# Own delays for the side steps of an emitted attention order, and wider tiles for the first adaLN weights

## The chip, the cores and the metric

The kernel runs on one core of one Trainium2 chip. The metric is the device time of one execution in microseconds (us). Within a core five engines work side by side: TensorE (PE, matrix products and transposes; its weight loads are listed apart as PEld), VectorE (DVE), ScalarE (ACT), GpSimd (POOL), and SyncE (SP), which in this kernel only issues transfers. Each engine works through its own list of instructions in order and waits at an instruction until what it needs is there.

## The reference, cut to what matters

Two layers of a hybrid backbone run over 640 tokens of width 1024: 128 context tokens and 512 latent tokens with shared weights. In each layer a conditioning vector is mapped to six modulation vectors (adaLN), one projection feeds three kinds of heads, and an output projection, a LayerNorm and an MLP follow.

```python
def _modulation(cvec, w_ada, b_ada):
    return jnp.split(jax.nn.silu(cvec) @ w_ada + b_ada, 6, axis=-1)
...
    h = x * (1.0 + sc_a) + sh_a
    mq, mk, mv, mo, mg, sq, sk, sv, nq, nk, nv = _split_in(h @ w_in + b_in)
    y_ml, _, _, _ = _mlstm_mixer(mq, mk, mv, mo, mg, fbias, norm_g, st_c, st_n, st_m)
    y_swa = _merge(_swa_latent(_rope_2d(_heads(sq, SWA_HEADS)), _rope_2d(_heads(sk, SWA_KV_HEADS)),
                               _heads(sv, SWA_KV_HEADS), ck_swa, cv_swa, sink))
    y_nat = _merge(_nat_latent(_heads(nq, NAT_HEADS), _heads(nk, NAT_HEADS), _heads(nv, NAT_HEADS),
                               ck_nat, cv_nat, rpb))
...
    mix = jnp.concatenate(mix_heads, axis=-1) @ w_out
    x = _layer_norm(DN_ALPHA * x + g_a * mix, ln1_g, ln1_b)
    h = x * (1.0 + sc_m) + sh_m
    f = jnp.square(jax.nn.relu(h @ w_mlp1)) @ w_mlp2
    return _layer_norm(DN_ALPHA * x + g_m * f, ln2_g, ln2_b)
```

The mLSTM scan carries a state from chunk to chunk, forward and backward; the context tokens hand their final state to the latent tokens. The outputs are both token streams, the context's keys and values, and the mLSTM states.

## The kernel before, in words

**Main stream.** Tokens are cut into five tiles of 128 (tile 0 is the context). Nearly all the work of TensorE is projections and MLP products: `gemm_feat` (L375, tile `gfeat`, features on the partitions) and `gemm_tok` (L306, tile `gtok`, tokens on the partitions). Every weight block arrives as `wrawt`, is split by ScalarE (L290) and VectorE (L291) into two parts `wst`, and each product is made of three matmuls.

**Side steps.** Everything else that TensorE does is cut into generators: the blocks of the neighbourhood heads (`nat`), of the window heads (`swa`) and of the mLSTM, the mLSTM's state recurrence (`chain`: `upd` L775, and on VectorE `mlst` L777), its closing (`finish`, `pty` L756), the context keys going out (`k_out`, `ptko` L863), the gates, the transposes back to features (`pth` L421), and adaLN (`ada`: load `adaw` L164, product `adaps` L169, bias add `adab` L183 on VectorE, transposes `adapt` L191). An attention block goes through scores `s` (L886), softmax on ScalarE and VectorE, transposes `ptp` (L929) and the product with the values `o` (L945).

**Order.** TensorE's list is written by hand. While the program emits the main stream it keeps a modelled time T; the steps lie in a queue with a ready time each, and after each piece of the main stream `pump` emits every eligible step whose ready time is not above T. The other engines' lists are set by a scheduler that follows data and buffers. All transfers are issued by SP in one list.

**First stage.** `start` computes the adaLN vectors that the first projection needs in four quarters. Each quarter takes eight 256 KB loads into eight `yp` buffers, its products, then the issue of the loads of the next quarter, which wait for these products to free the buffers.

**adaLN later on.** `ada` has one 1 MB buffer (`aw`), which `adaw`, the bias tile `adab` and the gate row share in turn. Each of the eight products of an `ada` is followed by the issue of the next load and a gap of modelled time; before the first product there is a load but no gap. In the MLP stages three of these run one after another.

**Output projection.** `tail1` makes it in two halves of 512 columns (`q` 0 and 1) with `by_block`: for each of eight row blocks k the tiles 0 to 2, later tiles 3 and 4, and the last block of all five at the end. The evacuation `ln_add` multiplies by the gate in place in PSUM (L1084) and adds to the residual `res` (L1088); the PSUM bank comes free with the second of these, and the second half needs the bank.

```python
            for k in range(7):
                blocks(k, range(3, NT))
            blocks(7, range(NT))
```

Of the kernel before, what the change touches and what calls it, by code (L numbers as in the profile page):

```python
# [9 lines left out]
F32 = mybir.dt.float32  # L10
# [20 lines left out]
YORDER = (0, 1, 5, 2, 6, 3, 7, 4)  # L31


class Net:
    def __init__(self, ctx, tc, I, O):
# [16 lines left out]
        self.queue, self.T = [], 0.0  # L52
# [11 lines left out]
    def add(self, gen, group, ready=0.0):  # L64
        self.queue.append([gen, group, max(self.T, ready)])
# [95 lines left out]
    def ada_load(self, pool, tag, l, i, q, n, k):  # L161
        w = pool.tile([128, 4, n], F32, tag=tag, name="adaw")
        src = self.I["w_ada0"][q, k] if l + i == 0 else self.I["w_ada"][3 * l + i - 1, q, k]
        self.nc.sync.dma_start(w, src.rearrange("p (j n) -> p j n", j=4))  # L164
        return w
# [32 lines left out]
    def ada(self, l, i, n, gap):  # L198
# [4 lines left out]
        ahead = [self.ada_load(self.adp, "aw", l, i, q, n, k) for q, k in todo[:1]]  # L203
        for m, (q, k) in enumerate(todo):
# [11 lines left out]
    def start(self):  # L216
# [5 lines left out]
        def load(q):  # L222
            w[q] = [self.ada_load(self.yp, "y", 0, 0, q, n, k) for k in range(8)]
# [75 lines left out]
    def gemm_tok(self, A, src, n, evac, by_block=False):  # L299
# [11 lines left out]
        if by_block:  # L311
# [24 lines left out]
            for k in range(7):  # L336
                blocks(k, range(3, NT))
            blocks(7, range(NT))
# [188 lines left out]
    def proj_ml(self, l, ms, pre=None):  # L527
# [11 lines left out]
        if ms[-1] == 3:  # L539
            self.ml_in = True  # L540
            self.ktok = self.yp.tile([128, 5, 256], F32, tag="y", name="ktok")
            self.add(self.ktok_prep(), "chain", self.use("A", 1.1, self.T + 0.3) + 0.1)
# [102 lines left out]
    def mlstm(self, l):  # L645
# [17 lines left out]
        def block(t):  # L663
# [67 lines left out]
            self.add(finish(t, hs), "fin", self.T + 2.4)  # L731
# [70 lines left out]
        for t in (0, 2, 3, 1, 4):  # L802
            self.add(block(t), "attn")
        self.add(chain(), "chain")
# [7 lines left out]
    def proj_qk(self, l, m, mode):  # L812
# [7 lines left out]
        if mode == "nk":  # L820
# [9 lines left out]
            self.add(self.k_out(kx, self.O["new_nat_k"][0, l, m - 4 : m - 2]), "kout", self.use("V", 0.3, f) + 0.1)  # L830
# [8 lines left out]
        else:  # L839
            for h in range(2):  # L840
                nc.scalar.activation(v[:, 0, h * 320 : (h + 1) * 320], g[h], AF.Identity, bias=b)
            if mode == "sk":
                kx = self.sm.tile([128, 128], F32, tag="kx", name="kxs", bufs=1)
                nc.vector.tensor_copy(kx, v[:, 0, 0:128])
                self.add(self.k_out(kx, self.O["new_swa_k"][0, l]), "kout", self.T + 2.5)
# [119 lines left out]
    def nat(self, l, u, qt, kt):  # L965
# [47 lines left out]
        for gen in [ctx_block()] + [block(cb) for cb in range(4)]:  # L1013
            self.s_left += 1
            self.add(gen, "attn", self.qk_ready)

    def swa(self, l, g, qt, kt, kc, vc):
# [52 lines left out]
        for gen in [ctx_block()] + [block(n) for n in range(4)]:  # L1070
            self.s_left += 1
            self.add(gen, "attn", self.qk_ready)
# [7 lines left out]
    def ln_add(self, r, q, o, gr, alpha, st=None):  # L1080
# [3 lines left out]
        nc.vector.tensor_tensor(out=o, in0=o, in1=gr[:, qs], op=ALU.mult)  # L1084
# [299 lines left out]
```

## Time and profile before

| | |
|---|---|
| median of 3 runs | 1780.16 us (1779.94 to 1780.73) |
| profiled execution | 1785.14 us |
| its span, first to last instruction | 1783.3 us |
| mean granted TensorE clock | 0.968 |
| TensorE busy | 1673.5 us (94% of the span) |
| VectorE busy | 958.7 us (54%) |
| ScalarE busy | 660.7 us (37%) |
| GpSimd busy | 187.8 us (11%) |

The time of the profiled execution and its span differ by 1.84 us, which lies around the recorded instructions. The first layer's attention runs from about 60 to 385 us, its MLP from about 415 to 940 us; the second layer's from about 945 to 1285 us and from about 1315 us to the end. The clock column of the profile is relative: 1.00 is TensorE's upper level of 2.4 GHz and 0.50 its lower of 1.2 GHz.

### The profile page before, as it was taken

What the parts mean: (1) busy time and instruction counts of PE and PEld (TensorE: products, weight loads), DVE (VectorE), ACT (ScalarE), POOL (GpSimd) and SP (SyncE); (2) the same over time, 40 slices, a digit from 0 to 9 for tenths busy, and PEclk for the clock granted to TensorE, in tenths of its full rate; (3) what the DMA queues carried; (4) which work ended last, traced back from release to release, by engine and by line L of the source; (5) the groups of instructions that cost most, each with busy time, mean ns of one, the idle gap of its engine ahead of it and who ended that gap; (6) DMA issues with size and microseconds to landing.
All of it is one profiled execution on the core that took longest, in us unless ns stands there. A gap on an engine that the chain in (4) does not pass through costs nothing.

```text
span 1783.3 us, 27709 instructions
## 1 busy us (share of the span) xinstructions
PE 1673.5 (94%) x10708; PEld 1453.3 (81%) x10708; DVE 958.7 (54%) x2105; ACT 660.7 (37%) x1482; POOL 187.8 (11%) x152
## 2 busy tenths in 40 slices
PE   5989898989999899999999897999899999999996
PEld 4879687868978777879988895888689898898985
DVE  3366766668633233234386787665685343433438
ACT  2342465645412212313253424666454142231320
POOL 1051000000201100101100510000003011020110
PEclk9998799999999999999999996999999999999998
DMA  8653442332344534422224331212413131321312
GB/s 280 223 157 122 165 131 90 106 119 78 108 152 159 172 130 165 166 78 94 63 77 143 106 110 36 64 58 76 130 60 104 50 101 43 105 78 53 98 45 83
DMA packets 107584, 195.24 MB, mean 109 GB/s; under 512 B 16666, under 2 KB 43290, under 8 KB 102332
## 3 DMA queue, kind: packets, MB, share of 16 engines
q1 hardware_dynamic: 107452, 193.47, 33.7%
q8 instruction: 84, 1.38, 0.3%
q14 instruction: 48, 0.39, 0.1%
HBM read 185.16 MB, written 8.26 MB: 108 GB/s over the span
## 4 chain that ended last, share of the span: by engine, by line
PE 75%; DVE 10%; DMA 5%; ACT 5%; issue 3%; SPq 0%; POOL 0%; DVEq 0%; ACTq 0%; POOLq 0%
PE gtok L306 34%; PE gfeat L375 31%; PE adaps L169 2%; ACT P L900 2%; PE o L945 2%; PE ptp L929 2%; DMA adaw<-in_w_ada 2%; DVE nm L893 2%; PE s L886 1%; PE mli L706 1%; DVE P L907 1%; DVE wst L291 1%; ACT PT L937 1%; DMA nbias<-in_nbias 1%; DMA adab<-in_b_ada 1%
## 5 line engine op out<-in xcount | busy, mean ns | idle before, releaser
L375 PE MATMUL gfeat<-Xt,wst 128*128 128x320 f32 x4416 | 688.1, 315 | 3.0 <-ACT f L1170 1.3
L375 PEld LDWEIGHTS gfeat<-Xt,wst 128*128 128x128 f32 x4416 | 660.6, 191 | 26.5 <-issue 16.6
L306 PE MATMUL gtok<-wst,f1T 128*128 128x512 f32 x1920 | 453.9, 397 | 1.8 <-POOL f1T L1175 1.2
L306 PEld LDWEIGHTS gtok<-wst,f1T 128*128 128x128 f32 x1920 | 361.6, 189 | 95.0 <-issue 7.5
L291 DVE TENSOR_TENSOR wst<-wrawt,wst 128x512 fp32r<-128x512 f32 (+2 forms) x392 | 272.8, 705 | 287.9 <-ACT wst L290 286.8
L290 ACT CAST wst<-wrawt 128x512 fp32r<-128x512 f32 (+2 forms) x392 | 232.5, 604 | 519.0 <-PE gtok L306 305.5
L1175 POOL TENSOR_TENSOR f1T<-f,f1T 128x640 fp32r<-128x640 f32 x64 | 103.4, 1615 | 1003.3 <-ACT f1T L1174 997.8
L1084 DVE TENSOR_TENSOR gtok<-gtok,row 128x512 f32<-128x512 f32 x100 | 69.4, 697 | 226.9 <-PE gtok L306 226.7
L306 PE MATMUL gtok<-wst,yT 128*128 128x512 f32 x480 | 120.3, 406 | 8.5 <-DVE res L1088 8.5
L306 PE MATMUL gtok<-wst,Xt 128*128 128x384 f32 (+1 forms) x720 | 122.1, 324 | 1.8 <-ACT wst L290 1.6
L306 PEld LDWEIGHTS gtok<-wst,Xt 128*128 128x128 f32 x720 | 113.0, 188 | 5.3 <-ACT wst L290 1.8
L306 PEld LDWEIGHTS gtok<-wst,yT 128*128 128x128 f32 x480 | 90.7, 193 | 30.4 <-DVE res L1088 9.4
L1170 ACT COPY f<-gfeat 128x320 f32<-128x320 f32 x128 | 54.3, 426 | 162.7 <-PE gfeat L375 158.0
L900 ACT ACTIVATE P<-P,nm 128x512 f32<-128x512 f32 (+2 forms) x120 | 80.6, 673 | 34.8 <-DVE nm L895 18.4
L169 PE MATMUL adaps<-adaw,cs 128*32 128x512 f32 (+1 forms) x576 | 60.0, 513 | 29.0 <-DMA adaw<-in_w_ada 28.3
L1171 DVE SCALAR_TENSOR_TENSOR f<-f 128x640 f32<-128x640 f32 x64 | 52.7, 823 | 52.7 <-ACT f L1170 52.7
L893 DVE TENSOR_REDUCE nm<-P 128x2 f32<-128x1024 f32 (+2 forms) x60 | 66.5, 1108 | 15.1 <-ACT P L982 8.5
L929 PE MATMUL ptp<-ident,P 128*128 128x128 f32 x432 | 65.5, 290 | 7.1 <-DVE P L907 5.9
L937 ACT COPY PT<-ptp 128x512 f32<-128x512 f32 (+1 forms) x120 | 60.9, 541 | 23.8 <-PE ptp L929 23.1
L424 ACT ACTIVATE val<-pth,affB,affA 128x128 f32<-128x128 f32 x120 | 45.5, 465 | 55.2 <-PE pth L421 55.2
L929 PEld LDWEIGHTS ptp<-ident,P 128*128 128x128 f32 x432 | 50.7, 147 | 16.9 <-issue 9.9
L1174 ACT CAST f1T<-f 128x640 fp32r<-128x640 f32 x64 | 46.6, 728 | 35.5 <-DVE f L1171 35.5
(208 smaller groups left out, 1282.4 us busy)
## 6 DMA issues: line engine op xcount, KB each, us to landing
wrawt<-in_w SPq DMA_DIRECT2D x256, 256.0 KB
adaw<-in_w_ada SPq DMA_DIRECT2D x40, 1024.0 KB
wrawt<-in_w_f SPq DMA_DIRECT2D x56, 256.0 KB
adaw<-in_w_ada SPq DMA_DIRECT2D x32, 256.0 KB
wrawt<-in_w_o SPq DMA_DIRECT2D x32, 256.0 KB
Dt<-md SPq DMA_DIRECT2D x40, 128.0 KB
nbias<-in_nbias SPq DMA_DIRECT2D x18, 256.0 KB
row<-adar SPq DMA_DIRECT2D x8, 512.0 KB
```

The source lines that it names most:

```text
L169: self.nc.tensor.matmul(ps[32 * j : 32 * j + 32, :], lhsT=self.cs[:, k, :], rhs=w[:, j, :], start=(k == 0), stop=(k == 7))
L290: nc.scalar.copy(ws[:, 0, :], raw)
L291: nc.vector.tensor_tensor(out=ws[:, 1, :], in0=raw, in1=ws[:, 0, :].bitcast(F32), op=ALU.subtract)
L306: nc.tensor.matmul(o, lhsT=A[YORDER[k] if A is self.Y else k][:, hl, t * 128 : (t + 1) * 128], rhs=ws[k][:, wl, :], start=(k == 0 and hl + ...
L375: nc.tensor.matmul(g[i, h], lhsT=w[i][k // 4][:, wl, (k % 4) * 128 : (k % 4 + 1) * 128], rhs=self.Xt[:, k, hl, h * 320 : (h + 1) * 320], s ...
L893: nc.vector.tensor_reduce(out=nm[:, 0:2], in_=P[:, :, 0:nk], axis=AX.X, op=ALU.max, negate=True)
L900: nc.scalar.activation(P[:, h, 0:nk], P[:, h, 0:nk], AF.Exp, bias=nm[:, h : h + 1], accum_out=nm[:, 2 + h : 3 + h])
L929: nc.tensor.transpose(pt[:, j, :], P[:, h, i * 128 : (i + 1) * 128], self.ident)
L937: nc.scalar.copy(dst, src)
L1084: nc.vector.tensor_tensor(out=o, in0=o, in1=gr[:, qs], op=ALU.mult)
L1170: nc.scalar.copy(f[:, h], g[h])
L1175: nc.gpsimd.tensor_tensor(out=y[:, 1], in0=f, in1=y[:, 0].bitcast(F32), op=ALU.subtract)
```

## The change

Four edits. (1) A table `LATER` of 63 named steps shifts the ready time of single steps, in tenths of a microsecond of modelled time; every step that is added gets a name (`0ml4` is layer 0, mLSTM, tile 4). (2) The first stage's adaLN weights are laid out so that one load brings two row blocks (512 KB instead of 256 KB) and a quarter takes four `yp` buffers instead of eight; the loads of quarter 1 are issued before quarter 0's products, those of quarter q+2 behind quarter q's. (3) `ada` yields once, for 8 us of modelled time, between its first load and its first product. (4) In the output projection the last block of tiles 0 to 2 comes as soon as its input is there, at the latest before the last block of tiles 3 and 4, and in the first half the gate product goes to an SBUF tile `wov`.

```diff
+LATER = {
+    "0": {7: -10, 8: 4},
...
+    "1ml4": {0: 102, 1: 27},
...
+    def add(self, gen, group, ready=0.0, name=""):
+        s = [gen, group, 0.0, f"{self.l}{name}", 0]
+        s[2] = max(self.T, ready) + self.later(s)
+        self.queue.append(s)
+
+    def later(self, s):
+        return 0.1 * LATER.get(s[3], {}).get(s[4], 0)
...
                         s[2] = max(self.T, ready)
+                        if cost > 0:
+                            s[4] += 1
+                            s[2] += self.later(s)
...
         ahead = [self.ada_load(self.adp, "aw", l, i, q, n, k) for q, k in todo[:1]]
+        yield 0.0, self.T + 8.0
         for m, (q, k) in enumerate(todo):
...
         def load(q):
-            w[q] = [self.ada_load(self.yp, "y", 0, 0, q, n, k) for k in range(8)]
+            w[q] = []
+            for k in range(4):
+                t = self.yp.tile([128, 2, 4, n], F32, tag="y", name="adaw")
+                nc.sync.dma_start(t, I["w_ada0"][q, k].rearrange("p (a j n) -> p a j n", a=2, j=4))
+                w[q] += [t[:, 0], t[:, 1]]
...
                 next(first)
+                load(1)
             for k in range(8):
                 self.ada_mm(ps[:, q, :], w[q][k], k)
-            if q < 3:
-                load(q + 1)
+            if q < 2:
+                load(q + 2)
...
-            for k in range(7):
+            late = True
+            for k in range(8):
                 blocks(k, range(3, NT))
-            blocks(7, range(NT))
+                if late and (k == 6 or (self.ydone[YORDER[7]] >= NT and self.yready[YORDER[7]] <= self.T)):
+                    late = False
+                    blocks(7, range(3))
...
-    def ln_add(self, r, q, o, gr, alpha, st=None):
+    def ln_add(self, r, q, o, gr, alpha, st=None, v=None):
...
-        nc.vector.tensor_tensor(out=o, in0=o, in1=gr[:, qs], op=ALU.mult)
+        v = o if v is None else v
+        nc.vector.tensor_tensor(out=v, in0=o, in1=gr[:, qs], op=ALU.mult)
+        o = v
...
-                self.ln_add(r, q, o, g[:, int(t == 0)], ALPHA, st[t] if q else None)
+                v = None if q else self.sm.tile([128, 512], F32, tag="val", name="wov", bufs=2)
+                self.ln_add(r, q, o, g[:, int(t == 0)], ALPHA, st[t] if q else None, v)
```

The names `L244`, `L266`, `L387`, `L459`, `L505` of the changed kernel are `L169`, `L191`, `L306`, `L375`, `L421` of the one before (the table pushes the lines down); `L767`, `L790`, `L796`, `L859`, `L947` are `L683`, `L706`, `L712`, `L775`, `L863`. In these lists a matmul on plain 32-bit floats stands once, where the trace has two records for it (`adaps` x4 there is x8 in the trace).

**First MLP, where one `ada` ends and the next begins (TensorE).** `adapt` are the last transposes of the first `ada`; the load of the next one is issued with them.

```order
L375 MATMUL gfeat<-Xt,wst 128x320 x60
L169 MATMUL adaps<-adaw,cs 32x512 x4
L375 MATMUL gfeat<-Xt,wst 128x320 x84
L191 MATMUL adapt<-ident,adab 128x128 x4
L375 MATMUL gfeat<-Xt,wst 128x320 x6
L169 MATMUL adaps<-adaw,cs 32x512 x4
```

The same place in the changed kernel:

```order
L459 MATMUL gfeat<-Xt,wst 128x320 x54
L244 MATMUL adaps<-adaw,cs 32x512 x4
L459 MATMUL gfeat<-Xt,wst 128x320 x78
L266 MATMUL adapt<-ident,adab 128x128 x4
L459 MATMUL gfeat<-Xt,wst 128x320 x72
L244 MATMUL adaps<-adaw,cs 32x512 x4
```

Between the transposes and the first product that needs the new load stood 6 matmuls of the main stream; now 72 stand there.

**First layer, the end of attention and the output projection (TensorE), before.** `o` is the last attention product, `pth` the transposes of a finished token tile; the first half of the output projection ends inside the long row.

```order
L945 MATMUL o<-PT,vc 64x128 x4
L306 MATMUL gtok<-wst,yT 128x512 x108
L421 MATMUL pth<-ident,res 128x128 x8
L306 MATMUL gtok<-wst,yT 128x512 x12
L421 MATMUL pth<-ident,res 128x128 x8
```

The same place in the changed kernel:

```order
L1029 MATMUL o<-PT,vc 64x128 x4
L387 MATMUL gtok<-wst,yT 128x512 x96
L505 MATMUL pth<-ident,res 128x128 x8
L387 MATMUL gtok<-wst,yT 128x512 x18
L505 MATMUL pth<-ident,res 128x128 x8
```

The number of products is the same; tiles 0 to 2 of each half are finished 12 matmuls sooner, and the transposes of their results come sooner with them.

**First layer, the mLSTM's recurrence (TensorE), before.** `mls` and `mli` are the block's products, `upd` the state updates, `ptko` transposes the context keys.

```order
L775 MATMUL upd<-mscr,ktok 64x65 x4
L375 MATMUL gfeat<-Xt,wst 128x320 x6
L775 MATMUL upd<-mscr,ktok 64x65 x4
L169 MATMUL adaps<-adaw,cs 32x512 x4
L863 MATMUL ptko<-ident,kxs 128x128
L375 MATMUL gfeat<-Xt,wst 128x320 x6
L706 MATMUL mli<-vaug,Dt 128x65 x4
L712 MATMUL mli<-mlst,mq 128x130 x4
L706 MATMUL mli<-vaug,Dt 128x65 x4
L775 MATMUL upd<-mscr,ktok 64x65 x4
```

The same place in the changed kernel:

```order
L859 MATMUL upd<-mscr,ktok 64x65 x4
L459 MATMUL gfeat<-Xt,wst 128x320 x6
L859 MATMUL upd<-mscr,ktok 64x65 x4
L459 MATMUL gfeat<-Xt,wst 128x320 x18
L790 MATMUL mli<-vaug,Dt 128x65 x4
L796 MATMUL mli<-mlst,mq 128x130 x4
L790 MATMUL mli<-vaug,Dt 128x65 x4
L859 MATMUL upd<-mscr,ktok 64x65 x4
L947 MATMUL ptko<-ident,kxs 128x128
L459 MATMUL gfeat<-Xt,wst 128x320 x18
L244 MATMUL adaps<-adaw,cs 32x512 x4
```

The transposes of the context keys and the `ada` product moved behind the block's products, and 18 main-stream matmuls instead of 6 stand ahead of these.

Further places of both attention stages move in the same way. One is on VectorE, where the bias add of a first-layer `ada` now stands between two steps of an mLSTM block (`num` is its numerator):

```order
L802 TENSOR_TENSOR num<-mli,mscr 128x260
L258 TENSOR_TENSOR adab<-adaps,adab 128x512
L803 TENSOR_TENSOR num<-num,mli 128x260
```

In the kernel before, the bias add stood among small steps of the gate norm and eight rows ahead of the first of that block's `num` rows.

## Rows read from the trace of the kernel before

**Rows 1.** The page: busy time and share by engine, and granted clock in 40 slices.

```profile
PE 1673.5 (94%) x10708; PEld 1453.3 (81%) x10708; DVE 958.7 (54%) x2105; ACT 660.7 (37%) x1482; POOL 187.8 (11%) x152
PEclk9998799999999999999999996999999999999998
```

**Rows 2.** The page: the chain that ended last, shares of the span by engine.

```profile
PE 75%; DVE 10%; DMA 5%; ACT 5%; issue 3%; SPq 0%; POOL 0%; DVEq 0%; ACTq 0%; POOLq 0%
```

**Rows 3.** Waits of PE: line, what ended them: total us, times, longest us.

```profile
PE adaps L169 <- DMA adaw<-in_w_ada: 28.3, 8, 7.8
PE gtok L306 <- DVE res L1088: 8.5, 2, 4.8
...
PE o L945 <- DVE yT L963: 5.5, 4, 4.1
PE ptko L863 <- DVE mlst L777: 5.3, 1, 5.3
PE pty L756 <- POOL hs L752: 5.1, 1, 5.1
...
PE gtok L306 <- POOL f1T L1175: 1.2, 1, 1.2
```

**Rows 4.** Windows at half clock: length, PE, PEld, DVE, ACT, POOL, clock, DMA, GB/s.

```profile
131.50:145.00 13.50, 12.15 (x57) 11.60 (x58) 8.11 (x33) 1.65 (x3) 3.06 (x5) 0.50 0.56 182
193.00:203.00 10.00, 10.00 (x57) 7.07 (x53) 6.19 (x18) 2.12 (x5) 0.00 (x0) 0.50 0.70 233
...
398.00:401.00 3.00, 3.00 (x9) 2.32 (x8) 3.00 (x7) 0.62 (x1) 0.00 (x0) 0.50 0.00 0
585.50:588.50 3.00, 3.00 (x15) 1.97 (x8) 0.00 (x0) 0.00 (x0) 0.00 (x0) 0.50 0.30 55
678.00:684.00 6.00, 5.80 (x17) 3.37 (x18) 0.00 (x0) 0.00 (x0) 0.00 (x0) 0.50 0.46 158
...
sum 94.00, PE 85.99 PEld 69.85 DVE 61.94 ACT 23.62 POOL 7.55; mean PE 5.37 PEld 4.37 DVE 3.87 ACT 1.48 POOL 0.47
```

**Rows 5.** Timeline, first MLP: start, duration, engine, operation, idle before and its releaser.

```profile
579.63 7.33 SPq L164 DMA_DIRECT2D adaw<-in_w_ada  x2
...
585.00 1.60 PE L169 MATMUL adaps<-adaw,cs 128*32 128x512 f32 x8 [4.53 <-DMA adaw<-in_w_ada]
...
596.55 1.06 PE L169 MATMUL adaps<-adaw,cs 128*32 128x512 f32 x8
...
678.20 1.94 PE L169 MATMUL adaps<-adaw,cs 128*32 128x512 f32 x8 [3.56 <-DMA adaw<-in_w_ada]
```

**Rows 6.** Timeline of PE, second layer: 72 main-stream matmuls in one row.

```profile
1338.69 11.05 PE L375 MATMUL gfeat<-Xt,wst 128*128 128x320 f32 x72 [0.52 <-ACT f L1170]
```

**Rows 7.** Timeline, first layer, between the halves of the output projection.

```profile
396.14 1.28 DVE L1088 SCALAR_TENSOR_TENSOR res<-res,gtok 128x512 f32<-128x512 f32 x2
...
397.47 2.78 PE L306 MATMUL gtok<-wst,yT 128*128 128x512 f32 x6 [4.83 <-DVE res L1088]
```

**Rows 8.** Timeline of PE, first stage: the first product of the second quarter.

```profile
18.60 1.31 PE L169 MATMUL adaps<-adaw,cs 128*32 128x128 f32 x16 [3.83 <-DMA adaw<-in_w_ada]
```

**Rows 9.** Waits of SP's list, 0 to 130 us: total us, times, longest us.

```profile
SPq L164 <- PE adaps L169: 17.8, 8, 4.5
```

**Rows 10.** Timeline of PE, first layer's attention: three gaps.

```profile
132.84 0.45 PE L863 MATMUL ptko<-ident,kxs 128*128 128x128 f32 x1 [1.92 <-DVE rsq L404]
...
191.97 1.10 PE L169 MATMUL adaps<-adaw,cs 128*32 128x512 f32 x8 [3.79 <-DMA adaw<-in_w_ada]
...
213.91 2.02 PE L929 MATMUL ptp<-ident,P 128*128 128x128 f32 x8 [1.92 <-DVE P L907]
```

**Rows 11.** Timeline of DVE, first layer's attention: a bias add that waited.

```profile
297.01 0.69 DVE L183 TENSOR_TENSOR adab<-adaps,adab 128x512 f32<-128x512 f32 x1 [3.57 <-DMA adab<-in_b_ada]
```

**Rows 12.** Windows over the two dense stretches of attention; columns as in rows 4.

```profile
187.00:221.00 34.00, 26.03 (x160) 17.98 (x158) 25.67 (x88) 14.30 (x41) 1.61 (x2) 0.70 0.44 146
...
1060.00:1115.00 55.00, 42.50 (x287) 36.52 (x287) 42.76 (x148) 21.87 (x60) 2.26 (x3) 0.75 0.20 60
```

More of the change, by code (lines that the diff above doesn't have):

```diff
@@ L31 @@
 YORDER = (0, 1, 5, 2, 6, 3, 7, 4)
+LATER = {
+    "0": {7: -10, 8: 4},
+    "0f2": {0: 10},
+    "0fin4": {0: 28},
+    "0g4": {0: 55, 1: -10},
+    "0ga": {0: 5},
+    "0ko10": {0: 25},
+    "0ko8": {0: 4},
+    "0ml1": {0: 5},
+    "0ml3": {0: 30, 1: -5},
+    "0ml4": {1: 11},
+    "0n00": {1: 5},
+    "0n01": {3: -5},
+    "0n02": {3: 3},
+    "0n03": {3: 5},
+    "0n10": {2: -3},
+    "0n12": {0: 7},
+    "0n13": {1: 5},
+    "0n14": {0: -10, 1: 16},
+    "0n21": {1: 17, 2: -10},
+    "0s00": {1: 16, 2: 11},
+    "0s01": {0: 88, 1: 17, 3: 25},
+    "0s02": {0: 36},
+    "0s03": {0: 38},
+    "0s10": {2: -3},
+    "0s11": {3: 18},
+    "0s12": {4: 4},
+    "0s14": {3: 3},
+    "0s21": {0: 30, 3: 8},
+    "0s22": {4: 30},
+    "0s23": {0: 15},
+    "0up": {5: 16},
+    "1f1": {0: 16},
+    "1f4": {0: 43, 1: 3},
+    "1fin0": {0: 8},
+    "1fin3": {0: 6},
+    "1fin4": {0: 54},
+    "1ko8": {0: 21},
+    "1kt": {0: -10},
+    "1ml0": {1: 34},
+    "1ml3": {0: -5},
+    "1ml4": {0: 102, 1: 27},
+    "1n01": {3: -3},
+    "1n02": {3: 20},
+    "1n03": {0: 10, 1: -10},
+    "1n04": {0: 10, 1: 5, 3: 33},
+    "1n10": {1: 10},
+    "1n20": {1: 30, 2: 20},
+    "1n21": {2: 5, 3: 32},
+    "1n22": {0: 6},
+    "1n23": {0: -10},
+    "1n24": {2: 5},
+    "1s00": {0: 18},
+    "1s01": {0: 13, 1: 3},
+    "1s02": {0: -5},
+    "1s03": {0: 52, 3: 30},
+    "1s04": {0: 10, 1: 8, 3: 10},
+    "1s10": {1: 3, 2: 20},
+    "1s11": {3: 4},
+    "1s12": {2: 5, 3: 10},
+    "1s13": {0: 20, 4: 9},
+    "1s14": {1: -5},
+    "1s20": {1: 5, 2: -3},
+    "1s21": {3: 11},
+    "1s22": {1: 20},
+    "1s24": {1: -2},
+}
 class Net:
@@ L51, in __init__ @@
         self.dr = pool("dr", 1, space=DRAM)
-        self.queue, self.T = [], 0.0
+        self.queue, self.T, self.l = [], 0.0, 0
         self.feat = [0] * NT
@@ L541, in proj_ml @@
             self.ktok = self.yp.tile([128, 5, 256], F32, tag="y", name="ktok")
-            self.add(self.ktok_prep(), "chain", self.use("A", 1.1, self.T + 0.3) + 0.1)
+            self.add(self.ktok_prep(), "chain", self.use("A", 1.1, self.T + 0.3) + 0.1, "kt")
     def ktok_prep(self):
@@ L730, in block @@
             self.busy["o"] = self.use("V", 1.3, self.busy["s"])
-            self.add(finish(t, hs), "fin", self.T + 2.4)
+            self.add(finish(t, hs), "fin", self.T + 2.4, f"fin{t}")
             yield 2.4, 0.0
@@ L802, in mlstm @@
         for t in (0, 2, 3, 1, 4):
-            self.add(block(t), "attn")
-        self.add(chain(), "chain")
+            self.add(block(t), "attn", 0.0, f"ml{t}")
+        self.add(chain(), "chain", 0.0, "up")
     def split_qk(self, src, dst):
@@ L1011, in block @@
                 self.live -= 2
-        for gen in [ctx_block()] + [block(cb) for cb in range(4)]:
+        for i, gen in enumerate([ctx_block()] + [block(cb) for cb in range(4)]):
             self.s_left += 1
-            self.add(gen, "attn", self.qk_ready)
+            self.add(gen, "attn", self.qk_ready, f"n{u}{i}")
     def swa(self, l, g, qt, kt, kc, vc):
@@ L1068, in block @@
                 self.live -= 2 if g == 2 else 1
-        for gen in [ctx_block()] + [block(n) for n in range(4)]:
+        for i, gen in enumerate([ctx_block()] + [block(n) for n in range(4)]):
             self.s_left += 1
-            self.add(gen, "attn", self.qk_ready)
+            self.add(gen, "attn", self.qk_ready, f"s{g}{i}")
     def rowbc(self, pool, tag, src):
@@ L1127, in f @@
                     self.feat[t] = 0
-                    self.add(self.to_feat(r, t, A, B), "feat", self.use("V", 2.5, f) + (0.5 if t < 3 else 5.0))
+                    self.add(self.to_feat(r, t, A, B), "feat", self.use("V", 2.5, f) + (0.5 if t < 3 else 5.0), f"f{t}")
             return f
@@ L1219, in f @@
                         self.feat[t] = 0
-                        self.add(self.to_feat(r, t, A, B), "feat", f + (0.5 if t < 3 else 5.0))
+                        self.add(self.to_feat(r, t, A, B), "feat", f + (0.5 if t < 3 else 5.0), f"g{t}")
                     else:
@@ L1245, in layer @@
         self.proj_tok_a(l)
-        self.add(self.gates(l), "chain", self.use("V", 0.6, self.T + 0.3))
+        self.add(self.gates(l), "chain", self.use("V", 0.6, self.T + 0.3), "ga")
         self.proj_ml(l, ML_SECOND)
```

13 lines of the change are left out of this document (6 added, 7 removed).

## The prediction, made before the changed kernel ran

> **What bounds the kernel now.** I read the page first: TensorE is busy 94% of the span, VectorE 54%, and the chain that ended last is TensorE for 75%, VectorE for 10%, transfers and ScalarE for 5% each [rows 1, 2]. The change removes no matmul, so the 1673.5 us of TensorE work stay and only two things can move: the roughly 110 us in which TensorE is idle (1783.3 less 1673.5), and the speed at which it runs. The clock row shows that the second is no small matter: most slices stand at 9 tenths or more, two of the first layer's attention at 8 and 7, one of the second layer's at 6 [rows 1].
>
> The list of TensorE's waits says where the idle time is. 28.3 us of it is one kind, an adaLN product that waits for its weights, in 8 places; 8.5 us is the start of the second half of the output projection, twice, which waits for VectorE to free PSUM banks; the waits of attention are single ones of 4 to 5 us [rows 3]. Then I went through the timeline for what follows each gap. The same eight adaLN products that take 1.06 us at one place take 1.60 and 1.94 us right behind a gap [rows 5], and windows laid behind the longer gaps show the granted clock at 0.50, its lower level, for 3 to 14 us each. In all there are 16 such windows, 94.0 us long, and TensorE is busy in 85.99 us of them; at the upper level that work would take about half, so some 43 us hang on the clock [rows 4].
>
> **The change part by part.** I sum against the profiled execution, 1785.14 us.
>
> *The pause before an `ada`'s first product.* In the first MLP two `ada` restart with 6 main-stream matmuls between the issue of the load and the product. The load is issued at 579.6 and is there at 585.0, so it takes 5.4 us, and TensorE waits 4.53 and 3.56 us [rows 5]. Now 72 matmuls stand between at the first place and 66 at the second. 72 of the same matmuls take 11.05 us elsewhere [rows 6], twice the load: both waits go, 8.1 us. Behind them the clock is low with 3.00 and 5.80 us of work [rows 4], half of which comes back, 4.4. Sum 12.5. Lower bound 8 (the clock falls for another reason); if a load took over 10 us the cover would be gone, and nothing here does.
>
> *The output projection.* The second half waits 8.5 us in two layers [rows 3]. At 397 us the last two of VectorE's eight evacuation steps, 1.28 us, end where TensorE restarts [rows 7]. Now tiles 0 to 2 are evacuated while TensorE still works on tiles 3 and 4 (six such matmuls take 2.78 us [rows 7]), and a bank is free after the first of two VectorE steps. I take both waits as gone, and half of the 3.00 us behind each: 8.5 + 2 x 1.5 = 11.5. The transposes `pth` come 12 matmuls sooner and may wait for their LayerNorm; 0.5 for it leaves 11. Bounds 6 and 11.5.
>
> *The first stage.* The second quarter's products wait 3.83 us for weights [rows 8], whose issue waits for products of the quarter before, 17.8 us in eight waits of SP's list [rows 9]. The new order issues quarter 1 ahead of quarter 0's products, in half as many issues. Transfers are busy in that stage too (first slices, and a first wait of 7.8 us that stays [rows 3]), so I take 3, between 0 and 7.
>
> The Trainium skill (DMA: Bandwidth & Descriptors, Rules for kernel authors) asks for at least 1 MiB per transfer for the full rate; by it 512 KB is still short of the mark; if the wider tiles brought nothing for that reason, this term would be 0 and the sum 42. No run here shows the rate against the size.
>
> *Before the last MLP product block.* A wait of 1.2 us for the MLP activation [rows 3] lies behind an `ada` bias add that held VectorE; it moves with the `ada`. 2 with its clock, bounds 0 and 3.
>
> *The delays in attention.* At 301 us `o` waits 4.1 us for VectorE [rows 3], which had itself waited 3.57 us in an `ada` bias add for its transfer [rows 11]. In the new order the attention block's output step stands ahead of that add instead of behind it: 4, bounds -1 and 5.
>
> In the first mLSTM stretch `ptko` waits 1.92 us [rows 10], and the clock is low over the next 13.5 us with 12.15 us of work [rows 4]. Now 18 matmuls instead of 6 stand ahead of the block's products, and `ptko` comes behind them. 1.9 and half of 12.15 make 8.0; one more VectorE wait of the recurrence may stay, so 6, bounds 0 and 8.
>
> In the first layer's dense stretch (187 to 221 us) the `ada` wait of 3.79 us goes behind other work and a softmax wait of 1.92 us should shrink [rows 10]; 10.00 us of work run at half clock there [rows 4]. All would be 3.8 + 1.9 + 5 = 10.7. But VectorE is busy 25.67 of 34 us [rows 12], so work that TensorE does sooner meets VectorE later. I take 5, bounds -2 and 10.7.
>
> In the second layer `ptko` waits 5.3 us for the recurrence [rows 3]. It moves behind the block's products, but the recurrence itself stays: 3, bounds 0 and 6. The dense stretch there (1060 to 1115 us) holds `pty`'s wait of 5.1 us [rows 3] and runs at 0.75 of the clock, but VectorE is busy 42.76 of 55 us [rows 12]. I take 3.5, bounds -2 and 10.6 (a quarter of the 42.50 us of work).
>
> *What is late next.* New orders make new waits. One is visible: a bias add stands between two steps of an mLSTM numerator on VectorE. If its bias is late by the 3.57 us of the row that shows such a wait [rows 11], the numerator, its normalisation and `pty` queue behind it. With a few smaller ones in so many moved places I set -5, bounds -10 and 0.
>
> Sum: 12.5 + 11 + 3 + 2 + 4 + 6 + 5 + 3 + 3.5 - 5 = 45. The profiled execution would be 1740.1 us; it is 5.0 above the median of the runs (1780.16), so I predict **1735 us**.
>
> **Rivals.**
>
> *Attention comes out even (chance 0.23).* For it: both dense stretches have VectorE at three quarters of the time, and VectorE's share does not change; against it: several of the waits are for a transfer or for an order on TensorE, not for VectorE's rate. What needs no luck is the `ada` pause, the projection, the first stage and the 2 us of the MLP: 28.5. 1785.1 - 28.5 - 5.0 = 1752.
>
> *The clock comes back nearly everywhere (0.12).* My sum holds about 17 of the 43 us at stake. If the shorter gaps leave the clock up through attention, the other 26 come on top: 1735 - 26 = 1709. Against it: in 193 to 203 us TensorE is busy all 10.00 us and the clock is still low [rows 4], so a closed gap alone does not bring it back at once.
>
> *Gaps close in attention, the clock stays low there (0.12).* The same row speaks for it: 10.00 us of work without a pause at 0.50 [rows 4]. Then the attention terms keep what their gaps give and lose the clock's part, which I put at three quarters of the 6, half of the 5 and 2 of the 3.5, or 9: 1735 + 9 = 1744. Against it: between these windows the clock is up in attention too, since the first dense stretch has 0.70 on the mean [rows 12].
>
> The Trainium skill (TensorE: Matmul & The Clock Gate, A second HAM failure mode: psum-queue depth-cycling) gives such a mechanism: short idles between groups of matmuls that cycle through PSUM banks keep the clock swinging, with no long gap. The row of 193 to 203 us agrees in that its 10.00 us at 0.50 hold no idle time, but it shows no swinging.
>
> *Slower (0.04).* The delays pull main-stream matmuls, the fill between attention steps, out of the dense stretches, and small products with short idles hold the clock at half throughout. Then 26.03 us at 0.70 become 36.4, and 42.50 at 0.75 become 63.8 [rows 12]: 31.7 more, and 5 for new waits, against the 28.5 that are sure: 1785.1 + 8.2 - 5.0 = 1788. It decides once the two stretches lose more than those 28.5 us. Against it: before, the clock was low in only part of either stretch, though their gaps were the longest.
>
> *The waits only move (0.03).* Each wait that goes is met by one as long: 1780. Against it: two `ada` waits and the bank wait have nothing late behind them.
>
> **How the numbers follow.** The forecast has 0.46, with a range of its own from 1722 to 1746. The rivals at 1752, 1744 and 1709 are all faster, so faster by over 0.2% (some 3.6 us, about what a measurement of this kernel can tell from no change) has 0.46 + 0.23 + 0.12 + 0.12 = 0.93; same 0.03; slower 0.04. For 8 in 10 the range goes down to 1714, which leaves out the best of the clock case, and up to 1762, which holds attention coming out even with 10 us of new waits on top.
>
> **What would show it.** Right: no `adaps` wait for weights over 1 us in the MLP stages, and no half-clock window there; no wait of `gtok` for L1088's successor between the halves; fewer than 60 us of windows at half clock in all; VectorE's busy time unchanged. The attention terms are wrong if the dense stretches are as long as before, the term for the recurrence if `ptko` or an `upd` still waits 5 us for it, the first stage if its last quarter ends where it did. The whole is wrong if the time is above 1765: then waits moved rather than went, or the clock is low over more of attention.

## The result and the profile after

The changed kernel takes 1753.12 us (median of 4 runs, 1749.54 to 1756.18) against 1780.05 us before: ratio 0.9849, 95% interval 0.9829 to 0.9869, so 1.5% or 26.9 us faster. Timed again later, the ratio was 0.9831 (0.9813 to 0.9849). The forecast was 1735 us, a gain of 45; the time lies in the range, between the forecast and the top of it.

Part of the distance is in what the sum was made against. The profiled execution of before stood 5.0 us above its median; that of after (1749.54) stands 3.6 below its own. Between these two executions the gain is 35.6 us. Single executions of one kernel spread by some 5 us to either side on the chips of the experiments, so a sum over one of them cannot be held to a few microseconds.

The page of the changed kernel, its lines for busy time, granted clock and the chain; they answer to [rows 1, 2]:

```profile
PE 1655.0 (95%) x10708; PEld 1439.3 (82%) x10708; DVE 954.8 (55%) x2105; ACT 660.0 (38%) x1482; POOL 189.8 (11%) x152
PEclk9999899999999999999999998999999999999998
PE 74%; DVE 11%; issue 5%; DMA 4%; ACT 4%; POOL 1%; SPq 0%; DVEq 0%; ACTq 0%; POOLq 0%
```

The 10708 matmuls are the same. TensorE's busy time fell by 18.5 us, which I read as speed, since the work is the same, and its idle time by 17.0 (from 109.8 to 1747.8 - 1655.0 = 92.8). The two make the 35.5 us of the span.

Where along the execution it came from is read from the start of the same instruction in both traces. The timeline of the changed kernel (start, duration, operation, idle before and its releaser):

```profile
386.67 2.59 PE L387 MATMUL gtok<-wst,yT 128*128 128x512 f32 x10 [0.78 <-DVE wov L1169]
...
916.92 1.06 PE L505 MATMUL pth<-ident,res 128*128 128x128 f32 x8 [1.48 <-DVE res L1303]
...
1249.34 1.89 PE L387 MATMUL gtok<-wst,yT 128*128 128x512 f32 x7 [0.78 <-DVE wov L1169]
...
1302.72 11.03 PE L459 MATMUL gfeat<-Xt,wst 128*128 128x320 f32 x72 [0.51 <-ACT f L1257]
```

And the kernel before, at the two of these places that stand in no row above:

```profile
942.02 1.06 PE L421 MATMUL pth<-ident,res 128*128 128x128 f32 x8 [1.95 <-DVE res L1216]
...
1284.14 2.12 PE L306 MATMUL gtok<-wst,yT 128*128 128x512 f32 x6 [3.71 <-DVE res L1088]
```

The second half of the first output projection starts 10.8 us sooner [rows 7], the end of the first MLP 25.1, the second projection's second half 34.8, the second MLP 36.0 [rows 6]. By stages, with what my terms make for the same stretch in brackets: from the start to the second half of the first projection 10.8 (21), the rest of that projection and the first MLP 14.3 (14.5), second attention up to the second half of its projection 9.7 (9.5), the rest about nothing. The first stretch is where the traces fall short. These are differences between one execution of each kernel. Where the order up to that place is the same, the second half of the first projection starts at 386.67, 389.02 and 391.20 us in three traces of the new order, and at 397.47 and 397.00 us in two of the old: gains of 6 to 11 us. So a figure by stage is uncertain by several microseconds, but none of these comes near 21.

TensorE's waits after; they answer to [rows 3]:

```profile
PE adaps L244 <- DMA adaw<-in_w_ada: 19.1, 7, 8.6
PE gtok L387 <- DVE wst L372: 7.4, 3, 4.0
...
PE gtok L387 <- DVE wov L1169: 1.6, 2, 0.8
```

The 8.5 us for which the second half of the projection waited for its PSUM bank are 1.6 now. The adaLN waits that are left, 19.1 us, all lie in the first 30 us. The waits of 5.3 us (`ptko`) and 5.1 us (`pty`, now 0.4 for the same releaser) are gone. New is the second line: main-stream matmuls wait for VectorE's weight split, 7.4 us in three places. New too are waits for `dn`, the denominator that VectorE makes for the mLSTM: 4.4 us of `mls`, 2.7 of `s` and 1.9 of `upd`.

The windows at half clock, two of the ten and their sum; they answer to [rows 4]:

```profile
144.50:151.50 7.00, 5.32 (x17) 5.32 (x18) 4.10 (x18) 0.43 (x2) 0.73 (x1) 0.51 0.27 66
...
1052.50:1069.50 17.00, 12.56 (x71) 10.22 (x72) 15.09 (x59) 5.01 (x18) 1.45 (x2) 0.50 0.21 69
...
sum 60.50, PE 49.82 PEld 41.62 DVE 52.08 ACT 19.56 POOL 6.31; mean PE 4.98 PEld 4.16 DVE 5.21 ACT 1.96 POOL 0.63
```

60.5 us and 49.8 us of work, where 94.0 and 86.0 were: half of the difference, 18.1 us, agrees with the fall of busy time by 18.5. Of the 60.5 us, 17 are one window in the second attention; its like in the kernel before lies from 1073.5 to 1090.5 us and is as long. The last 8 to 10 us of either kernel, in which TensorE has no work left, stand in neither sum.

### The profile page after: what moved, and what is told of

The parts are those of the page before. It is cut to its first block, busy times and chain, and to the rows that moved or that the text cites. A ratio compares the mean times of both kernels' runs of the same rounds, so it can differ in the third digit from the quotient of the medians.

```text
span 1747.8 us, 27703 instructions
## 1 busy us (share of the span) xinstructions
PE 1655.0 (95%) x10708; PEld 1439.3 (82%) x10708; DVE 954.8 (55%) x2105; ACT 660.0 (38%) x1482; POOL 189.8 (11%) x152
## 4 chain that ended last, share of the span: by engine, by line
PE 74%; DVE 11%; issue 5%; DMA 4%; ACT 4%; POOL 1%; SPq 0%; DVEq 0%; ACTq 0%; POOLq 0%
PE gtok L387 34%; PE gfeat L459 30%; PE adaps L244 2%; PE o L1029 2%; PE ptp L1013 2%; ACT P L984 2%; PE s L970 1%; DMA adab<-in_b_ada 1%; DVE nm L977 1%; DVE wst L372 1%; DVE P L991 1%; DMA wrawt<-in_w_f 1%; DMA adaw<-in_w_ada 1%; PE mli L790 1%; POOL f1T L1262 1%
## 5 line engine op out<-in xcount | busy, mean ns | idle before, releaser
L459 PE MATMUL gfeat<-Xt,wst 128*128 128x320 f32 x4416 | 682.0, 313 | 6.6 <-ACT Xt L509 3.1
L459 PEld LDWEIGHTS gfeat<-Xt,wst 128*128 128x128 f32 x4416 | 655.2, 190 | 27.4 <-issue 11.6
L387 PE MATMUL gtok<-wst,f1T 128*128 128x512 f32 x1920 | 452.6, 396 | 0.9 <-ACT wst L371 0.8
L387 PEld LDWEIGHTS gtok<-wst,f1T 128*128 128x128 f32 x1920 | 359.1, 188 | 96.0 <-issue 8.4
L1169 DVE TENSOR_TENSOR gtok<-gtok,row 128x512 f32<-128x512 f32 x90 | 62.8, 698 | 226.5 <-PE gtok L387 226.1
L387 PE MATMUL gtok<-wst,Xt 128*128 128x384 f32 (+1 forms) x720 | 125.9, 330 | 7.4 <-DVE wst L372 7.4
L387 PEld LDWEIGHTS gtok<-wst,Xt 128*128 128x128 f32 x720 | 116.3, 193 | 11.3 <-DVE wst L372 8.6
L387 PE MATMUL gtok<-wst,yT 128*128 128x512 f32 x480 | 117.8, 399 | 1.6 <-DVE wov L1169 1.6
L387 PEld LDWEIGHTS gtok<-wst,yT 128*128 128x128 f32 x480 | 88.3, 188 | 22.9 <-DVE wov L1169 2.4
L244 PE MATMUL adaps<-adaw,cs 128*32 128x512 f32 (+1 forms) x576 | 56.1, 497 | 19.2 <-DMA adaw<-in_w_ada 19.1
```

Source lines behind the costliest of these rows:

```text
L244: self.nc.tensor.matmul(ps[32 * j : 32 * j + 32, :], lhsT=self.cs[:, k, :], rhs=w[:, j, :], start=(k == 0), stop=(k == 7))
L387: nc.tensor.matmul(o, lhsT=A[YORDER[k] if A is self.Y else k][:, hl, t * 128 : (t + 1) * 128], rhs=ws[k][:, wl, :], start=(k == 0 and hl + ...
L459: nc.tensor.matmul(g[i, h], lhsT=w[i][k // 4][:, wl, (k % 4) * 128 : (k % 4 + 1) * 128], rhs=self.Xt[:, k, hl, h * 320 : (h + 1) * 320], s ...
L1169: nc.vector.tensor_tensor(out=v, in0=o, in1=gr[:, qs], op=ALU.mult)
```

## Experiments

Each was timed in turn with the kernel before, whose median on these chips was 1782.88 or 1783.88 us; a gain is what the ratio makes of that median. The interval of a gain is plus or minus 3 to 4 us where only a few runs stand behind it and 2 to 3 where a dozen do. Three chips were used: one for the pause, the projection, the wider tiles and the emptied table, a second for the first-layer delays, quarter 1, the split and the changed kernel again, a third for the delayed transposes, the delays alone and both further edits; times of different chips are compared by their ratios only.

**The pause alone, in the second layer's `ada`.**

```diff
+        if l == 1:
+            yield 0.0, self.T + 8.0
```

> The kernel before with one part of the change alone: the pause of 8 us of modelled time before an ada's first product, and only for the ada of the second layer, which run in the first MLP; attention's order is untouched. My theory: both restart waits (4.53 and 3.56 us) go and the two windows at half clock behind them with them, so 12.5 us less, 1767.5 us; the page shows no adaLN wait over 1 us after 400 us. The rival, that the wait or the low clock turns up elsewhere in the MLP: 1772 to 1780 us, with a new gap in that stage.

Measured: 1770.17 us, ratio 0.9938 (0.9917 to 0.9959), 11.1 us. The theory holds: no adaLN wait after 400 us is left. In the changed kernel the place reads so (it answers to [rows 5]):

```profile
572.78 0.60 PE L266 MATMUL adapt<-ident,adab 128*128 128x128 f32 x4
573.13 10.80 PE L459 MATMUL gfeat<-Xt,wst 128*128 128x320 f32 x72
583.86 1.06 PE L244 MATMUL adaps<-adaw,cs 128*32 128x512 f32 x8
```

The 72 matmuls hide the load, and the product takes 1.06 us, its time at the full clock, not 1.60.

**The output projection alone.** The edit is that part of the diff.

> The kernel before with the edit of the output projection alone (last block of tiles 0 to 2 earlier, gate product of the first half into SBUF); the order differs only there. My theory: both waits between the halves fall from 8.5 us in all to under 2 and the half-clock windows behind them go, 10 to 11 us less, 1769 to 1770 us. The rival, that a later wait takes their place (transposes of the finished tiles wait for their LayerNorm): 4 to 6 us less, 1774 to 1776 us.

Measured: 1774.33 us, ratio 0.9963 (0.9948 to 0.9978), 6.6 us. That is between the two. The timeline of this kernel, second layer, shows both:

```profile
1278.21 12.01 PE L306 MATMUL gtok<-wst,yT 128*128 128x512 f32 x50 [0.78 <-DVE wov L1088]
...
1322.66 1.06 PE L424 MATMUL pth<-ident,res 128*128 128x128 f32 x8 [3.21 <-DVE res L1132]
1323.48 10.58 PE L378 MATMUL gfeat<-Xt,wst 128*128 128x320 f32 x60
```

The bank wait fell from 3.71 to 0.78 us, but the last transposes wait 3.21 us for the LayerNorm (1.47 before), and the clock is low behind them, in windows of this trace from 1323 to 1328 us. The profiled execution, 1781.06 us, is the slowest of its twelve; but two further runs without the second layer's delays (the emptied table and the first-layer delays below) have the same wait, 3.3 and 3.8 us, with a low clock behind it.

**The same, with three of the transposes delayed.**

```diff
-                    self.add(..., self.use("V", 2.5, f) + (0.5 if t < 3 else 5.0))
+                    self.add(..., self.use("V", 2.5, f) + (0.5 if t < 3 else 5.0)
+                             + {(0, 2): 1.0, (1, 1): 1.6, (1, 4): 4.3}.get((l, t), 0.0))
```

> The kernel before with the edit of the output projection, as in the run of that edit alone, and with the transposes of three finished tiles delayed (1.0 us in the first layer, 1.6 and 4.3 us in the second, the table's own numbers for these steps). That run gained 6.6 us where the prediction had 11; its trace has a wait of 3.2 us for the LayerNorm's result in the second layer with a window at half clock behind it. If that wait is the shortfall: it goes, and the gain is 10 to 11 us, ratio 0.994. If not: 6 to 7 us as before, ratio 0.996.

Measured: 1773.48 us, ratio 0.9940 (0.9925 to 0.9956), 10.7 us. In its trace the last of these transposes wait no longer:

```profile
1318.43 1.03 PE L424 MATMUL pth<-ident,res 128*128 128x128 f32 x8
```

So the forecast's 11 fits the edit with this wait out of the way, and the table of the changed kernel holds these three delays. The intervals of the two runs overlap a little, and they are of two chips, so that the wait is the whole shortfall is likely rather than proven.

**The wider first tiles alone.**

> The kernel before with the wider first adaLN tiles alone; TensorE's order is the same, only the transfers differ. The prediction's step: 3 us less, 1777 us, by shorter waits for weights in the first 30 us. The rival from the trace of the changed kernel: two weight loads that wait for a buffer stand between the first and the second load of quarter 1 in SP's list, so quarter 1 ends no sooner; what is left is that later loads start 4 us sooner, worth 0 to 2.6 us: 1777.5 to 1780 us, with TensorE's second wait in the first 30 us longer, not shorter, than 3.84 us.

Measured: 1782.89 us, ratio 1.0003 (0.9989 to 1.0017): nothing. The rival was right, and the reason is in SP's list of the changed kernel:

```profile
14.40 0.43 SPq L302 DMA_DIRECT2D adaw<-in_w_ada  x1
18.89 0.93 SPq L369 DMA_DIRECT2D wrawt<-in_w_f  x2
19.87 1.37 SPq L302 DMA_DIRECT2D adaw<-in_w_ada  x3
```

One load of quarter 1 goes out, then two projection weights wait until 18.89 us for a buffer that VectorE's weight split has to free, and the other three of quarter 1's four loads stand behind them. TensorE, same kernel (the first line answers to [rows 8]; the second wait is the longer one that the rival foretold):

```profile
18.81 1.08 PE L244 MATMUL adaps<-adaw,cs 128*32 128x128 f32 x16 [4.04 <-DMA adaw<-in_w_ada]
25.58 1.08 PE L244 MATMUL adaps<-adaw,cs 128*32 128x128 f32 x16 [5.68 <-DMA adaw<-in_w_ada]
```

Nor did the wider loads move fewer bytes in the same time: from 30 to 46 us the changed kernel moves 410 GB/s, the one before 306, though the gaps between their issues differ too.

**Quarter 1 ahead of the projection's weights** (in the changed kernel).

```diff
             if q == 0:
+                load(1)
                 first = self.gemm_feat(...)
                 next(first)
-                load(1)
```

> The changed kernel with the loads of quarter 1 issued ahead of the first projection's weight loads; TensorE's order is the same. My theory, that SP's list held quarter 1 behind two weight loads that wait for a buffer until 18.9 us: the wait at 25.6 us (5.7 us) shrinks to under 2 and the first main-stream matmul starts 3 to 4 us sooner than at 29.7, so 3 us under the changed kernel. The rival, that the stage is bound by the bytes it moves: the projection's weights come later instead, the first main-stream matmul starts at 29 to 30 us and the time is that of the changed kernel.

Measured: 1749.68 us, ratio 0.9821 (0.9799 to 0.9843), where the changed kernel on the same chip has 1752.88 and 0.9831: 3.2 us by the medians, 1.8 by the ratios, within what the intervals allow for nothing. The trace is clearer than the time:

```profile
15.68 1.08 PE L244 MATMUL adaps<-adaw,cs 128*32 128x128 f32 x16 [0.81 <-DMA adaw<-in_w_ada]
...
23.69 0.90 PE L459 MATMUL gfeat<-Xt,wst 128*128 128x320 f32 x2 [2.27 <-ACT wst L371]
```

Both long waits go and the first main-stream matmul starts at 23.69 us, not 29.72; then the projection waits for its own weights (2.27), and 2 to 3 of the 6 us are left by 100 us. By the second half of the first projection nothing is left of them in these two traces (386.86 us against 386.67). Both theories were half right.

**The table emptied** (in the changed kernel, `LATER = {}`).

> The changed kernel with the table of delays emptied; the other three edits stay, and with them the pause in the ada of the first layer. If the delays are worth what the prediction put on attention (18.5 less 5, some 13.5 us): 1766 us. The rival, that the time came from the other three edits (15 in the first MLP, 6 in the projections, 2 to 3 in the first stage) and the delays gave under 5: 1753 to 1758 us. If it is over 1770 us, the other edits alone worsen attention and the delays mend that.

Measured: 1765.46 us, ratio 0.9913 (0.9894 to 0.9933): the other three edits give 15.5 us, the delays the other 11 to 15 (against the changed kernel's ratios of 0.9849 and 0.9831). That holds the forecast's net figure for attention, 13.5, but some 4 of it are likely the three transposes of the projections, which leaves 7 to 11 for attention itself. The trace shows what the delays are set against. In the first layer's dense stretch it has two waits that the kernel before does not have:

```profile
192.48 1.97 PE L725 MATMUL mli<-vaug,Dt 128*128 128x65 f32 x8 [4.85 <-DVE P L1074]
...
218.78 0.69 PE L775 MATMUL pty<-ident,hs 128*128 128x128 f32 x2 [4.93 <-POOL hs L771]
```

At the first of these places the kernel before waits 3.79 us for `ada` weights [rows 10]. The pause, the only edit left that moves TensorE's steps there, takes that wait away, and one for VectorE stands in its place; in the changed kernel both of these are gone.

**The first layer's delays only** (the keys that begin with 1 left out).

> The changed kernel with the delays of the second layer taken out of the table, those of the first kept. With the whole table the kernel measured 27 us under the one before, with an empty one 15.5. If the delays work by themselves in each layer, and the second layer's share is the prediction's 6.5 of 18.5: some 4 us slower than the changed kernel. The rival from the traces, that the first layer's gain went into new waits (VectorE's weight split, 4.0 us) and most of the 11.5 us is the second layer's: 8 to 11 us slower.

Measured: 1762.13 us, ratio 0.9882 (0.9865 to 0.9900), 9 us slower than the changed kernel on that chip. By the times the rival is nearer: 9 of 11 to 15 us are the second layer's, where I had put the smaller share; some 4 of them are likely the transposes of that layer's projection, by the run that delays these. The traces do not settle it. Between the emptied table and the full one, 6.9 of 12.5 us are there by the second half of the first projection (393.52 and 386.67 us), and the trace of this run, whose order up to that place is the changed kernel's own, gets there at 391.20. One execution differs from another by nearly as much as the share in question, so the split between the layers stays open.

**The delays alone** (the table on the kernel before).

> The kernel before with the table of delays alone; no pause, no wider tiles, the output projection as before. If the delays work by themselves: 11 to 12 us under the kernel before, what emptying the table cost the changed kernel (ratio 0.9935). The rival, that they are fitted to the order that the other edits make (the pause moves each adaLN step of the first layer): under 5 us, ratio 0.997 to 1.0, with waits in the first layer as long as before.

Measured: 1780.03 us, ratio 0.9980 (0.9967 to 0.9992), 3.6 us (1.4 to 5.9). The rival was right: the same table is worth 11 to 15 us on top of the other edits and about 4 without them. In the first layer of its trace the `ada` wait stays (3.70 us at 190 us), a wait for the weight split of 3.25 us is new, and the second half of the projection starts at 400.26 us, no sooner than before (397.47). In the second layer the waits of `ptko` and `pty` are gone. The parts alone (11.1, 6.6, 0 and 3.6) make 21, the whole 27 to 30; the pause alone was tried in the second layer's `ada` only.

**The weight split of one projection on GpSimd** (in the changed kernel).

```diff
+        self.split = nc.gpsimd
         self.gemm_tok(self.X, I["w_tc"][l], 384, ev)
...
-        nc.vector.tensor_tensor(out=ws[:, 1, :], in0=raw, in1=..., op=ALU.subtract)
+        self.split.tensor_tensor(out=ws[:, 1, :], in0=raw, in1=..., op=ALU.subtract)
```

`self.split` is VectorE for every other projection.

> The changed kernel with the weight split of one projection (the values of the neighbourhood heads, 8 pieces per layer) on GpSimd instead of VectorE; TensorE's order is the same. My theory, that the new waits for the split (4.0 us at 146, 2.4 and 1.0 at 1016) come from VectorE's list being full there: they go, with the low clock behind them, 5 to 9 us under the changed kernel. The rival, that GpSimd is slower or busy with the mLSTM's own steps and only passes the wait on: within 2 us of the changed kernel, or slower, with waits for GpSimd in their place.

Measured: 1749.13 us, ratio 0.9812 (0.9792 to 0.9831), 3.4 to 3.8 us under the changed kernel (ratios, medians), below the 5 to 9 expected and again within the intervals; the wait itself is settled by the trace. In the changed kernel VectorE goes from one instruction to the next, busy for all of the 12.10 us from 134.0 to 146.1, and the split that TensorE waits for is the last of this row:

```profile
144.77 0.81 DVE L894 TENSOR_TENSOR qkt<-qkv,qkt 128x640 fp32r<-128x640 f32 x1
145.51 0.16 DVE L485 TENSOR_SCALAR rsq<-hst 128x4 int32<-128x4 int32 x1
145.57 0.55 DVE L372 TENSOR_TENSOR wst<-wrawt,wst 128x384 fp32r<-128x384 f32 x1
```

TensorE waits 4.04 us for it at 146 us. With the split on GpSimd, 36 of these matmuls run without a gap, and the window at half clock is gone:

```profile
142.04 6.51 PE L389 MATMUL gtok<-wst,Xt 128*128 128x384 f32 x36
```

Most of what was gained there was lost again. Against the changed kernel's trace this one is 3.7 us ahead at 186 us; then a wait for VectorE's `dn` takes 3.8 us instead of 2.7, and at the second half of the projection the lead is 1.0 us (385.67 against 386.67). In the second layer an `upd` of this kernel waits 4.8 us for `dn`, 1.9 in the changed one. The two spans differ by 1.3 us.

**Both further edits together.**

> The changed kernel with both further edits: quarter 1's loads ahead of the first projection's weights, and the weight split of the neighbourhood heads' values on GpSimd. TensorE's order is the changed kernel's. If the two gains (3.2 and 3.8 us on the medians) are of separate places, they add up: ratio 0.979 to 0.980 to the kernel before, some 6 to 7 us under the changed kernel, with neither wait in the trace. The rival, that a later wait of attention (the clock in its dense stretches, or VectorE) takes a gain made earlier: 0.981 to 0.983, no better than either alone.

Measured: 1749.55 us, ratio 0.9804 (0.9786 to 0.9822). Not decided: the ratio lies between the two expectations and the interval holds both. In its profiled execution the first stage has a new low window:

```profile
23.00:34.00 11.00, 9.12 (x31) 7.97 (x32) 6.24 (x10) 4.18 (x8) 1.55 (x1) 0.53 0.85 302
```

The run with the loads alone, which has the same edit in that stage, has none there.

**The changed kernel again.**

> The changed kernel itself, on the same chip as the other three: 27 us under the one before, ratio 0.985. If its gain depends on where the clock falls in attention, its runs spread over 5 us and more, as those of the kernel before did.

Measured: 1752.88 us, ratio 0.9831. The gain was 30.1 us on this chip, more than the 27 expected but within the interval; its four runs spread over 2.0 us only, so a spread of 5 us and more did not show.

## Why the prediction was right, and where it was not

**The sum.** The time lies in the stated range, 18 us above the forecast. In the traces the gain is 35.5 us of the 45, and nearly all of that difference is in the stretch up to the second half of the first projection, 10.8 of 21; the other 8.6 us are how far the two profiled executions stand from their medians. The step that failed is that the terms were added as if each edit kept its worth beside the others: what needed no luck, 28.5, measured 15.5 without the delays, and the delays, 13.5 net, measured 11 to 15 beside the other edits but 3.6 alone. That the delays came near their 13.5 is partly luck: they got it in part by taking away waits that the pause and the projection's edit had made.

**The pause.** Right in mechanism and size: 12.5 expected, 11.1 measured, interval 7.3 to 14.8. The wait of 1.2 us before the last MLP block is gone from the list of the changed kernel; the 2 us put on it cannot be told apart within that error.

**The output projection.** Mechanism right, size wrong: 11 expected, 6.6 measured. The step that failed is "The transposes `pth` come 12 matmuls sooner and may wait for their LayerNorm; 0.5 for it". That wait was 3.2 us with a low clock behind it; delayed transposes give 10.7. In the changed kernel the table delays them, so the term came out nearly whole, but by an edit that the forecast had not counted for it: that is luck.

**The first stage.** Wrong: 3 expected, 0 measured. The step that failed is that "the new order issues quarter 1 ahead of quarter 0's products". The line of code stands there, but behind the weights of the first projection, which wait for buffers, and SP issues in order. The row of SP's list that said so, two weight loads at 18.88 us, was in the trace of before as well; I had read the wait for the products and not this one. And I had read that wait wrongly: of the 17.8 us of [rows 9], taken over 0 to 130 us, only 0.3 lie before 32 us. The sign that I had named against the term came true: the last quarter's products end at 46.05 us, before at 45.93.

**The first layer's attention.** Expected 4 + 6 + 5, less half of the new waits; the traces came to about half or less. Single waits went as foreseen: `o` waits 0.9 us where it waited 4.07, and `ptko` at 131 us waits for nothing. What failed is the size and the place of "What is late next". I had put a bias add first. It did wait, 3.38 us at 176.08, and TensorE's next `mls` behind it 2.36 us. But the dearer wait was the weight split at 146 us, 4.04 us with 5.32 us of work at half clock behind it, close behind where the new order saves the wait at 133 us [rows 10]: VectorE was full there, and TensorE, having come sooner, waited for it. The first layer's delays bring this wait: it is 4.40 us with these delays alone in the table and 0.31 with the table empty. Moving the split off VectorE removed it, which shows the cause of the wait. That it is most of the shortfall is not shown: with the wait gone, the next waits for VectorE took most of the gain, and 1.0 us was left at the end of the stretch. In the dense stretch behind it the `ada` wait of 3.79 us is gone, but waits of 2.71, 1.50 and 2.31 us for VectorE stand from 190 to 206 us, and TensorE's idle time over 187 to 221 us is 7.7 us, where it was 8.0. Which of these costs how much stays open.

**The second layer's attention.** About right: with its half of the projection 9.5 expected, 9.7 in the traces; from one pair of executions, so that it agrees to 0.2 us is luck. The waits of `ptko` and `pty` both went, more than the half I had allowed, and new ones of 1.9 to 2.4 us for VectorE's `dn` and `wst` came. The window of 17 us at half clock, which the kernel before has too, stayed; it is longer than the 3 to 14 us that the forecast gives for such windows.

**Rivals.** The time, 1753, is that of "attention comes out even", 1752, but its cause is not: attention did not come out even, since the delays gave 11 to 15 us, some 7 to 11 of it in attention, while the other edits gave less than the rival counts on. "Gaps close in attention, the clock stays low there" does not hold for the first dense stretch either way: its gaps did not close, and its clock on the mean (187 to 221 us) rose from 0.70 [rows 12] to 0.80, though a window of 10 us at half clock stayed. It holds for the window of 17 us in the second layer's.

**The signs.** No adaLN wait is left in the MLP stages and no half-clock window while TensorE works there, no `ptko` or `upd` waits 5 us for the recurrence, and VectorE's busy time is 954.8 us, nearly unchanged, all as foretold. Between the halves of the projection 0.78 us remains, for `wov`. The windows at half clock make 60.5 us, just above the 60 that I had named as the limit.

What the clock adds to the noise is seen where TensorE's order is the same in three kernels: the stretch between the last two `pty` of the second layer's dense part, in the kernel before, with the projection edit, and with the wider tiles, one line from each trace.

```profile
1091.20:1107.10 15.90, 8.07 (x60) 6.01 (x60) 14.30 (x49) 9.77 (x28) 0.72 (x1) 0.80 0.06 18
```

```profile
1086.20:1104.30 18.10, 10.82 (x62) 8.39 (x60) 14.24 (x49) 9.87 (x28) 0.72 (x1) 0.59 0.07 16
```

```profile
1086.60:1102.60 16.00, 8.09 (x60) 6.07 (x60) 14.38 (x49) 9.82 (x28) 0.72 (x1) 0.80 0.07 18
```

The same work (two matmuls at the window's edge are counted in the second) takes 2.1 to 2.2 us more where the clock is 0.59. What tips it there is open.

**Still open.** How the 10 us and more that the first layer fell short divide among its new waits, how the delays' worth divides between the layers, whether the two further edits add up, and what an earlier load of the bias tile would give; the latter was not tried, for want of a free buffer.

## What to carry to other kernels

A wait that is covered by work already in the list (the pause, the bank) gave here about what its row says, the low clock behind it included. A line of code moved ahead is not a transfer moved ahead: read the issuing queue's own list for what stands between and what that waits for. And where a stretch has its second engine full, a new order may save TensorE's waits only until the next thing that this engine has to deliver, here the weight split and then `dn`; look for that before adding up the gaps. Terms of edits that move the same steps do not simply add up.

## What the runs showed that was not expected

A table of delays is worth 3.6 us alone and 11 to 15 us beside the edits that it was set against; one of these, the pause, makes waits of nearly 5 us in the first layer that the table then takes away. The same instructions in the same order ran at a mean clock of 0.59 or 0.80 from one execution to another, which alone moves the time by 2 us in one stretch.
